# Layer 0's modulation as TensorE sums in 32-column groups, and another order of the steps ahead of the channel mixing

## The chip, the cores and the metric

The kernel runs on one core of a Trainium2 chip. The metric is the device time of one execution in microseconds (us); a kernel's time is the median of several executions. A core has five engines that run side by side, each with its own queue of instructions in program order: TensorE (PE; its weight loads are shown as PEld), VectorE (DVE), ScalarE (ACT), GpSimd (POOL) and SyncE (SP, which here only issues loads and stores). An instruction that waits holds up all that stand behind it on its engine.

## What is computed

A two-layer backbone over 512 latent tokens of 1024 features, with 256 context tokens, in f32. Every layer begins with a modulation: a vector made of the condition `c` (and for the context of `c_ctx`) by a 1024 x 6144 matrix, cut into six chunks of 1024 features: shift, scale and gate of the mixer, then of the MLP.

```python
s_lat = jax.nn.silu(c)
s_ctx = jax.nn.silu(c_ctx)
for i in range(DEPTH):
    mod_l = [m[:, None, :] for m in jnp.split(s_lat @ ada_w[i] + ada_b[i], N_MOD, axis=-1)]
    a_lat = _modulate(_rmsnorm(h_lat, norm1_g[i]), mod_l[0], mod_l[1])      # h * (1 + scale) + shift
    if i % 2 == 0 or ctx_live:
        mod_c = jnp.split(s_ctx @ ada_w[i] + ada_b[i], N_MOD, axis=-1)
        a_ctx = _modulate(_rmsnorm(h_ctx, norm1_g[i]), mod_c[0], mod_c[1])
    ...
    h_lat = h_lat + mod_l[2] * y_lat
    h_lat = h_lat + mod_l[5] * _sq_relu_mlp(
        _modulate(_rmsnorm(h_lat, norm2_g[i]), mod_l[3], mod_l[4]), mlp_w1[i], mlp_w2[i])
return _rmsnorm(h_lat, final_g)
```

`y_lat` is the mixer's output: in layer 0 differential attention beside a Hyena long convolution, in layer 1 a pooling mixer. So layer 0 needs all six chunks for the latent tokens, and chunks 0 and 1 for the context as well.

## The kernel before

Everything is feature-major: tiles of 128 features (partitions) by 512 tokens. Large products are made of f32r parts: each operand is split into a high part (a ScalarE cast) and a low part (a subtraction on VectorE or GpSimd), and three products are summed (`mm3`, `proj_steps`: high x high, high x low, low x high). Products of the modulation are plain f32; TensorE runs each of those as two instructions.

**Stages.** First the start: the Hyena filter's network and spectrum (`fm`, `ft`, `tp`, `fo`, `kp`, `ks`), layer 0's modulation, and the norm and modulation of x (`sq`, `aq`, `xn`, `xm`, then the parts `xh` and `xl`). Then layer 0's mixer: projections (`u`, four products a step, six steps a unit, weights loaded by `x` and split by `w` and `r`), values (`vm`), context keys (`kx`), scores and softmax (`S`, `M`, `E`, `C`), the weighted values (`T`, `H`, `L`, `V`), the transforms of the long convolution (`F`, `I`), and the first output products (`X`). Last the channel mixing: output projection, the MLP of layer 0, the pooling mixer and the MLP of layer 1, one weight tile of 128x1024 after the other.

**What sets the order.** Ahead of the channel mixing the order is written out by hand: the lists START and MIDDLE name one step after another, and `play` emits them; each engine runs its own instructions in that order. A step's name is that of its function, then its number, then sometimes a letter for the engine of an elementwise step (v: VectorE, g: GpSimd). Data dependences and buffers that are still in use become waits.

**Layer 0's modulation.** `sil` holds silu of the condition (columns 0 to 7) and of the context's constant (8 to 15). For the first 512 features of chunks 1 and 0, both streams go over TensorE: `gemv` (`gv`, L594) takes the two columns of one feature tile as stationary operand and 512 weights as moving one, two products a step, eight steps, into two accumulators of two rows; `ga` copies them, `gt` transposes them to columns, `gm` adds bias and gain. All other features go over VectorE: a row step multiplies 128 rows of the transposed weights (`adaT`, 128x1024) by the condition, broadcast over the partitions (`sbc`, made by `sb` and `sc`), and sums along the row (L637: eight `gr` steps in the start; L649: 32 `rw` steps in the mixer, of which eight are the context's). Each is followed by one or two one-column steps for bias and gain (`gf`, `rf`; L250, L255, L660, L665). Chunk 5 of layer 0 and all of layer 1 are such rows in the channel mixing (`grow`, L1472): 8 + 48 of them, one or two after each MLP tile.

The weight tiles and rows come by `lg` and `lr`, half a megabyte each, on SP's queue; the `sraw` ring of four buffers is shared by `lr` rows, raw projection weights (`x`) and later loads. PSUM has two accumulators each of the kinds `mm` and `tr` (512 columns) and two wide ones, `sc` (1024 columns), for filter taps, spectra, scores and the inverse transform.

Of the kernel before, what the change touches and what calls it, by code (L numbers as in the profile page):

```python
# [9 lines left out]
F32 = mybir.dt.float32  # L10
# [8 lines left out]
P = 128  # L19
# [24 lines left out]
MIDDLE = """
ca4g w2 r2 kw3 cs0 j0 sc3 k0 l0 rw0 lr2 nw0 lr3 x3 u12 u13 u14 cr0 rw1 u15 x4 u16 j1 k1 lv0 lr4 w3 rf1 cp0 rf0 rw2
u17 cn0 rw3 r3 ck0 cx2v cx3v cm2 lr5 u18 u19 u20 u21 u22 rf3 cx6v j2 rf2 w4 cx7v rw4 k2 lr6 x5 cx4 rw5 rf5 rf4 r4 l1
l2 cx0 u23 u24 u25 cx5v cm4 cm3 j3 w5 u26 u27 cx1 rw6 u28 k3 rf6 lr8 rw8 rf8 cm0 cm1 x6 lr7 r5v cm6 ch3 rw7 u29 u30
u31 u32 u33 u34 rf7 x7 lr9 ch2 cl2g l3 lb0 ch0 j4 ch6 w6 k4 cl0 x8 rw9 r6 cm7 w7 r7 u35 vm0 vm1 vm2 vm3 lr12 lr10
lr11 j5 k5 ch1 rf9 va0 cl3 vm4 vm5 vm8 cl6 rw10 rf10 vm6 vm7 ch4 w8 cl1 ch7 va1 vh0 cm5 cl4g r8 vm9 rw11 rf11 rw12
rf12 vm10 ch5 cl5 vm12 x9 vm11 cl7g vl0g va2 lr13 w9 vh1 r9 lr14 lr15 x10 w10 vm13 vm14 vm15 vh2 vm16 rw13 lr20 lo0  # L50
rf13 lr18 va3 vm17 vm18 vm19 lr16 vm20 vm21 rw14 rf14 va4 rw15 lr17 lr19 vh3 vm24 vm25 vm26 x11 vm27 lr21 va6 rf15
lr22 x12 vm22 vm23 va5 l4 vl1g vl2g vl3 vm28 vm29 vm30 vh6 vm32 vm31 rw16 vl6 va7 vh7 vm33 vm34 vh4 vm35 va8 r10
rf16 rw17 vl7g vm36 rf17 vm37 vm38 vm39 rw18 rf18 va9 vh5 vm40 rw19 rf19 rw20 rf20 vm41 vh8 vm44 vm45 l5 vl4 vm42
vl5g vm43 vh9 vm46 w11 va10 vm47 u60 u61 vl8g va11 rw21 rf21 rw22 r11 vl9 rf22 vh10 lr24 lr28 lr23 lr25 u62 u63 u64
u65 ka0 lr26 kb0 rw23 km0 rf23 kx0 u66 u67 kx1 u68 u69 u70 u71 w12 ky0 r12 rw24 kd0 rf24 rw25 vl10g kh0 rw26 u72 ka1
kb1 rf25 km1 x13 lr27 x14 x15 lr29 kl0 rw27 rf26 u73 kx2 kx3 u74 u75 u76 kx4 u77 vh11 w13 ky1 r13 kd1 kh1 kl1g rf27
rw28 rf28 kx5 ka2 kb2 ky2 lr30 lr31 rw29 rf29 la0 la1 w14 le0 u78 u79 u80 u81 u82 u83 vl11g km2 r14 rw30 ln0 kd2
rw31 q0 s0 t0 u84 u85 u86 kx6 u87 u88 kh2 w15 kl2 r15 a0 rf30 b0 c0 rf31 b1 c1g u89 kx7 ka3 kb3 km3 S0 M0 x20 x17
u90 u91 S1 M1 u92 S3 kd3 u93 S2 u94 u95 x16 E0 w16 ky3 E1 kh3 r16 kl3g M3 C0 M2 q1 E2 s1 u96 T0 H0 E3 w17 L0 t1 r17
C1 u97 u98 u99 S5 u100 a1 M5 S4 u101 M4 u102 T1 u103 u104 S6 E5 j16 k16 x19 x18 w18 H1 L1 V0 S7 E4 C2 T2 u105 M6 M7  # L60
u106 b2 b3 O0 c2 H2 E7 E6 L2 C3 u107 c3v Q0 r18 u108 S8 f0 f1 T3 u109 M8 j17 H3 L3 w19 E8 S9 u110 u111 M9 k17 E9 Q2
f2 l16 l17 f3 Q3 S10 V1 u112 S11 M10 C4 T4 E10 Q5 r19 O1 M11 E11 H4 w20 S12 M12 u113 q2 u114 u115 Q1 u116 S13 u117
N0 C5 L4 s2 t2v R0 M13 W0 r20 T5 u118 u119 B0 H5 E13 L5 a2 D0 z1 x21 w21 x22 V2 U0 j19 b5 E12 k19 f4 l19 C6 G0 c5 Q4
v0 O2 b4 S14 u120 u121 S15 u122 T6 y0 M14 E14 Q7 c4 H6 K0 f5v p1 r21 M15 E15 L6 u123 u124 u125 S16 C7 S17 M16 M17 T7
q3 s3 x23 u126 u127 u128 U1 E16 H7 L7 V3 E17 w22 v1 C8 O3 t3v Q8 f6 y1 a3 b7 f7v S18 M18 u129 S19 T8 H8 u130 M19 E18
E19 L8 u131 N1 U3 r22 Q6 p0 R1 C9 v3 w23 S20 U2 F2 S21 W1 v2 j21 T9 y3 M20 y2 k21 r23 E20 b6 M21 P2 H9 E21 L9 z0 S23
# [1955 lines left out]
```

## Time and profile before

| | |
|---|---|
| median of the runs shown (3) | 1159.12 us (1159.09 to 1161.04) |
| span of the profiled execution | 1157.6 us |
| TensorE busy | 1098.5 us (95%) |
| VectorE busy | 729.7 us (63%) |
| ScalarE, GpSimd busy | 442.8 us (38%), 455.5 us (39%) |
| loaded and stored | 165.6 MB |

The time outside the span is 1.5 us against the median. Busy shares over the whole span mix stages with different limits: the start and the mixer take the first 352 us, the channel mixing the other 806. So the trace is read by stage, and inside a stage by what ended an engine's idle time. On TensorE a product's listed duration includes the time until its last column is out; products that follow each other overlap in this, so the distance of two starts tells what a product costs in a row of them.

### The profile page before, as it was taken

To read this page: it belongs to the slowest core of one execution; us is meant where nothing else is said; L and a number is where in the kernel's file an instruction comes from. 1 tells how busy PE (TensorE), PEld (TensorE's weight loads), DVE (VectorE), ACT (ScalarE), POOL (GpSimd) and SP (SyncE) were. 2 spreads that over 40 slices of the span, in tenths; PEclk is the share of its full clock that TensorE was granted. 3 is DMA by queue.
4 is the path that set the end of the run, shared out by engine and by line. 5 is a ranking of instruction groups with operands and counts; after the bars stand their busy time and mean duration, and the time that the engine had idled before them with its cause. 6 is when DMAs were issued, how large, how long until landed. Compare 5 with 4: busy or idle time off the path is not lost.

```text
span 1157.6 us, 14600 instructions
## 1 busy us (share of the span) xinstructions
PE 1098.5 (95%) x5624; PEld 917.5 (79%) x5624; DVE 729.7 (63%) x1080; ACT 442.8 (38%) x747; POOL 455.5 (39%) x325
## 2 busy tenths in 40 slices
PE   8788987999999999999999999989999999999996
PEld 2467976787789987888888888989888888888886
DVE  5889887899984768578577666576522332332334
ACT  3555224666535443143133133366422422322331
POOL 5858757655664413113113212356131131231212
PEclk9899998999999899999999999989999999999998
DMA  9577743102625237656646644221231332322302
GB/s 351 206 249 239 246 170 129 55 20 82 186 91 198 74 113 274 232 165 223 242 155 227 224 164 164 73 74 50 97 114 69 110 109 73 109 101 81 105 5 73
DMA packets 49802, 165.55 MB, mean 143 GB/s; under 512 B 5378, under 2 KB 8706, under 8 KB 49604
## 3 DMA queue, kind: packets, MB, share of 16 engines
q1 hardware_dynamic: 47284, 154.13, 38.6%
q0 software_dynamic: 2448, 10.49, 2.7%
q8 instruction: 44, 0.72, 0.3%
q14 instruction: 26, 0.21, 0.1%
HBM read 160.40 MB, written 4.20 MB: 142 GB/s over the span
## 4 chain that ended last, share of the span: by engine, by line
PE 73%; DVE 15%; POOL 4%; ACT 3%; issue 3%; DMA 2%; SPq 0%; POOLq 0%; DVEq 0%; ACTq 0%
PE r L199 11%; PE r L196 10%; PE r L194 10%; PE f L199 9%; PE f L196 9%; PE f L194 9%; PE v L897 2%; DVE mx L1074 1%; DVE g L649 1%; DVE e L1094 1%; DMA g<-in_adaT 1%; PE f L1631 1%; DVE g L637 1%; DVE nl L1530 1%; DVE ks L985 1%
## 5 line engine op out<-in xcount | busy, mean ns | idle before, releaser
L163 POOL TENSOR_TENSOR wlo<-raw,whi 128x1024 fp32r<-128x1024 f32 x77 | 194.7, 2531 | 527.0 <-ACT whi L162 384.8
L196 PE MATMUL r<-gl,whi 128*128 128x512 f32 (+1 forms) x576 | 207.1, 368 | 2.1 <-DVE gl L1622 2.1
L162 ACT CAST whi<-raw 128x1024 fp32r<-128x1024 f32 x135 | 139.7, 1041 | 179.3 <-PE r L196 151.9
L194 PE MATMUL r<-gh,whi 128*128 128x512 f32 (+1 forms) x576 | 207.3, 368 | 0.0
L194 PE MATMUL f<-nh,whi 128*128 128x512 f32 (+1 forms) x512 | 191.4, 379 | 0.0
L196 PE MATMUL f<-nl,whi 128*128 128x512 f32 (+1 forms) x512 | 191.1, 378 | 0.0
L1543 DVE SCALAR_TENSOR_TENSOR h<-r,mods,h 128x512 f32<-128x512 f32 (+1 forms) x81 | 54.4, 671 | 163.8 <-PE r L199 163.6
L1621 DVE TENSOR_TENSOR r<-r 128x512 f32<-128x512 f32 (+1 forms) x72 | 53.8, 748 | 150.4 <-ACT gh L1620 150.3
L199 PE MATMUL r<-gh,wlo 128*128 128x512 f32 (+1 forms) x576 | 130.2, 368 | 0.0
L1619 ACT ACTIVATE r<-f 128x512 f32<-128x512 f32 (+1 forms) x72 | 39.5, 549 | 236.7 <-PE f L199 235.0
L196 PEld LDWEIGHTS r<-gl,whi 128*128 128x128 f32 x576 | 108.4, 188 | 21.5 <-DVE gl L1622 2.5
L194 PEld LDWEIGHTS r<-gh,whi 128*128 128x128 f32 x576 | 108.3, 188 | 19.2
L199 PE MATMUL f<-nh,wlo 128*128 128x512 f32 (+1 forms) x512 | 121.3, 379 | 0.0
L1472 DVE CUSTOM_DVE_ANT_0 g<-g,sbcl 128x1024 f32<-128x1024 f32 x56 | 117.4, 2097 | 1.7 <-DMA g<-in_adaT 1.7
L199 PEld LDWEIGHTS r<-gh,wlo 128*128 128x128 f32 x576 | 100.5, 188 | 18.9
L194 PEld LDWEIGHTS f<-nh,whi 128*128 128x128 f32 x512 | 96.2, 188 | 19.0
L196 PEld LDWEIGHTS f<-nl,whi 128*128 128x128 f32 x512 | 96.3, 188 | 18.8
L199 PEld LDWEIGHTS f<-nh,wlo 128*128 128x128 f32 x512 | 92.3, 188 | 18.9
L163 DVE TENSOR_TENSOR wlo<-raw,whi 128x1024 fp32r<-128x1024 f32 x58 | 75.9, 1308 | 9.5 <-ACT whi L162 9.5
L194 PE MATMUL u<-ah,whi 128*128 128x512 f32 x160 | 67.0, 419 | 9.5 <-ACT whi L735 4.3
L196 PE MATMUL u<-al,whi 128*128 128x512 f32 x160 | 65.4, 409 | 0.3 <-POOL al L719 0.3
L744 POOL TENSOR_TENSOR wlo<-raw,whi 128x1024 fp32r<-128x1024 f32 x19 | 48.4, 2546 | 9.9 <-ACT whi L735 7.0
(372 smaller groups left out, 1948.5 us busy)
## 6 DMA issues: line engine op xcount, KB each, us to landing
raw<-in_w SPq DMA_DIRECT2D x128, 512.0 KB, 4.4
g<-in_adaT SPq DMA_DIRECT2D x96, 512.0 KB, 4.4
raw<-in_w_hy SPq DMA_DIRECT2D x12, 512.0 KB, 3.9
g<-in_adaN SPq DMA_DIRECT2D x8, 512.0 KB, 8.5
raw<-in_w_qk SPq DMA_DIRECT2D x8, 512.0 KB, 3.5
pth<-in_pth POOLq DMA_DIRECT2D x4, 768.0 KB, 7.8
raw<-in_w_out SPq DMA_DIRECT2D x5, 512.0 KB, 3.6
x<-in_xT SPq DMA_DIRECT2D x8, 256.0 KB, 10.8
```

The lines of the kernel that those rows point to most:

```text
L162: act.copy(out=hi, in_=src)
L163: (lo_eng or dve).tensor_tensor(out=lo, in0=src, in1=f32(hi), op=ALU.subtract)
L194: pe.matmul(ps, wh[:, c], ah[i][:, t0 : t0 + n], start=(i == 0), stop=False)
L196: pe.matmul(ps, wh[:, c], al[i][:, t0 : t0 + n], start=False, stop=False)
L199: pe.matmul(ps, wl[:, i * P : (i + 1) * P], ah[i][:, t0 : t0 + n], start=False, stop=(i == k - 1))
L637: dve.tensor_tensor_reduce(out=g, in0=g, in1=sbc[0], scale=1.0, scalar=0.0, op0=ALU.mult, op1=ALU.add, accum_out=mods[:, 0, c, d : d + 1])
L744: ew(pool if k else dve).tensor_tensor(out=wts[k][1], in0=raws[k], in1=f32(wts[k][0]), op=ALU.subtract)
L897: pe.matmul(pp[:, :256], a, b, start=(k == 0 and e == 0), stop=(k == ND - 1 and e == 2))
L1472: dve.tensor_tensor_reduce(out=gin[k], in0=gin[k], in1=sbc[0], scale=1.0, scalar=0.0, op0=ALU.mult, op1=ALU.add, accum_out=mods[:, layer, ...
L1543: dve.scalar_tensor_tensor(out=hs[d][:, seg], in0=pp[:, :n], scalar=gate[:, d : d + 1], in1=hs[d][:, seg], op0=ALU.mult, op1=ALU.add)
L1619: act.activation(out=r, in_=pp[:, :n], func=AF.Relu)
L1621: dve.tensor_tensor(out=r, in0=r, in1=r, op=ALU.mult)
```

## The change

Layer 0's modulation goes over TensorE entirely. The stationary operand is now 32 columns wide (`sil2`, in which the columns of one feature tile's condition and context stand side by side, and whatever follows them fills the other thirty), and a step multiplies one feature tile (128 rows of the weights in their own layout, `adaN`) by 2048 weights: four products of 512 columns, each into another group of 32 partitions of one accumulator (`gemv_tile`). Eight steps `gv` make chunks 1 and 0 of both streams; sixteen steps `rv` in the mixer make chunks 2 and 3 (`rv0` to `rv7`), then 4 and 5 (`rv8` to `rv15`) in the two halves of one wide `sc` accumulator, which they keep until `ra1` and `ra0` have copied it. `gt` and `rt` transpose a copied accumulator by four 128x128 blocks; `gm` and `rm` add bias and gain for eight tiles at a time. The steps `gr`, `gf`, `rw`, `rf` are gone, and so are the context's broadcast condition and the eight rows of chunk 5 in the channel mixing (`gq`). The condition's broadcast is still made, for layer 1's rows.

START has 213 steps in place of 232, MIDDLE 826 in place of 870; nearly all stand in another place, and some 60 elementwise steps are on another engine (eleven weight low parts `r` go from GpSimd to VectorE, three modulations of x, `xm`, from ScalarE to VectorE). In the new lists the first `u` stands behind `xl0`, thirteen `kp` steps and the first two weight splits (`w0`, `w1`); `rv0` to `rv3` stand among the first six units, `rv4` to `rv11` among the values, `rv12` to `rv14` ahead of the first scores, `rv15` behind the second ones. `proj_steps` and `v_unit` look their weights' parts up later, so that a part may be emitted between two of a unit's steps.

```diff
+    sil2 = per.tile([P, 48], F32, name="sil2", tag="sil2")
+    sil = sil2[:, 0:16].rearrange("p (k s) -> p s k", s=2)
+    e16 = sil2[:, 16:32]
+    nhalf, ones = sil2[:, 32:36], sil2[:, 40:41]
+    dve.memset(sil2[:, 32:48], -0.5)
...
-    gtt = [(c, d) for d in range(4, ND) for c in (1, 0)]
...
-        if k < ND:
-            nc.sync.dma_start(out=gts[k], in_=I["adaN"][k])
-        else:
-            c, d = gtt[k - ND]
-            nc.sync.dma_start(out=gts[k], in_=I["adaT"][0, c * D + d * P : c * D + (d + 1) * P, :])
+        nc.sync.dma_start(out=gts[k], in_=I["adaN"][k // 2, :, k % 2, :])
...
-        nc.sync.dma_start(out=rows_in[k], in_=I["adaT"][0, c * D + j * P : c * D + (j + 1) * P, :])
+        nc.sync.dma_start(out=rows_in[k], in_=I["adaN"][k % 16 // 2, :, 2 + 2 * (k // 16) + k % 2, :])
...
+    gav, gas, gat = {}, {}, {}
+    def gemv_tile(dst, k, srcs):
+        for b in range(4):
+            pe.matmul(
+                dst[32 * b : 32 * b + 32, :], sil2[:, 2 * k : 2 * k + 32], srcs[b // 2][:, b % 2 * T : (b % 2 + 1) * T],
+                start=(k == 0), stop=(k == ND - 1),
+            )
+    def gemv_copy(r, src):
+        gas[r] = m3.tile([P, T], F32, name=nm("gas"), tag="P", bufs=4)
+        act.copy(out=gas[r], in_=src)
+    def gemv_columns(r):
+        t = ps_tr("gat")
+        for i in range(4):
+            pe.transpose(t[:, i * P : (i + 1) * P], gas[r][:, i * P : (i + 1) * P], idn)
+        gat[r] = t.rearrange("p (i c h s) -> p s c h i", i=4, c=2, h=2)
+    def by_half(ap):
+        return ap.rearrange("p (h i) -> p h i", h=2)
     @step("gv")
     def gemv(k):
-        for c in range(2):
-            pe.matmul(
-                lazy(gav, c, lambda: ps_tr("gav"))[0:2, :], sil.rearrange("p (s k) -> p k s", s=2)[:, k, :],
-                gts[k][:, c * T : (c + 1) * T], start=(k == 0), stop=(k == ND - 1),
-            )
+        gemv_tile(lazy(gav, 0, lambda: ps_tr("gav")), k, (gts[2 * k], gts[2 * k + 1]))
     @step("ga")
-    def gemv_out(c):
-        gas[c] = m3.tile([2, T], F32, name=nm("gas"), tag="P", bufs=4)
-        act.copy(out=gas[c], in_=gav[c][0:2, :])
+    def gemv_out(_):
+        gemv_copy(0, gav[0])
     @step("gt")
     def gemv_t(_):
-        gat.append(ps_mm("gat"))
-        for i in range(8):
-            pe.transpose(gat[0][:, 2 * i : 2 * i + 2], gas[i // 4][:, i % 4 * P : (i % 4 + 1) * P], idn[0:2, 0:2])
+        gemv_columns(0)
     csm = per.tile([P, ND], F32, name="csm", tag="csm")
     @step("gm")
     def first_mods(k):
-        gr = gat[0][:, 0:16].rearrange("p (c d s) -> p c s d", c=2, s=2)
-        dst_s, dst_m = ((smul[:, 0, 0:4], mods[:, 0, 0, 0:4]), (csm[:, 0:4], cmods[:, 0, 0:4]))[k]
-        dve.tensor_tensor(out=dst_s, in0=gr[:, 0, k, :], in1=gpre[:, 0, 0:4], op=ALU.add)
-        dve.tensor_tensor(out=dst_s, in0=dst_s, in1=pr("n1g", 0, 4), op=ALU.mult)
-        dve.tensor_tensor(out=dst_m, in0=gr[:, 1, k, :], in1=pr("ada_b", 0, 4), op=ALU.add)
+        gr = gat[0][:, k]
+        dst_s, dst_m = ((smul[:, 0, :], mods[:, 0, 0, :]), (csm, cmods[:, 0, :]))[k]
+        dve.tensor_tensor(out=by_half(dst_s), in0=gr[:, 0], in1=by_half(gpre[:, 0, :]), op=ALU.add)
+        dve.tensor_tensor(out=dst_s, in0=dst_s, in1=pr("n1g", 0, ND), op=ALU.mult)
+        dve.tensor_tensor(out=by_half(dst_m), in0=gr[:, 1], in1=by_half(pr("ada_b", 0, ND)), op=ALU.add)
+    rav = {}
+    @step("rv")
+    def row(n):
+        r, k = n // ND, n % ND
+        acc_ = lazy(rav, 0, lambda: ps_sc("rav"))[:, r * T : (r + 1) * T]
+        gemv_tile(acc_, k, (rows_in[2 * n], rows_in[2 * n + 1]))
+    @step("ra")
+    def row_out(r):
+        gemv_copy(1 + r, rav[0][:, r * T : (r + 1) * T])
+    @step("rt")
+    def row_t(r):
+        gemv_columns(1 + r)
+    @step("rm")
+    def row_mods(r):
+        gr = gat[1 + r][:, 0]
+        o = (2 + 2 * r) * ND
+        if r == 0:
+            pairs = ((mods[:, 0, 2, :], 0), (mods[:, 0, 3, :], 1))
+        else:
+            pairs = ((mods[:, 0, 5, :], 1),)
+            dst = smul[:, 1, :]
+            dve.tensor_tensor(out=by_half(dst), in0=gr[:, 0], in1=by_half(gpre[:, 1, :]), op=ALU.add)
+            dve.tensor_tensor(out=dst, in0=dst, in1=pr("n2g", 0, ND), op=ALU.mult)
+        for dst, c in pairs:
+            dve.tensor_tensor(
+                out=by_half(dst), in0=gr[:, c], in1=by_half(pr("ada_b", o + c * ND, o + (c + 1) * ND)), op=ALU.add
+            )
...
-        sbps[n] = bcast(ps, "mm" if n < 2 else "tr", sil[:, n * 4 : n * 4 + 4], 4, "sb")
+        sbps[n] = bcast(ps, "tr", sil[:, 0, n * 4 : n * 4 + 4], 4, "sb")
...
-        act.copy(out=(sbc[0] if n < 2 else sbc_c)[:, n % 2 * T : (n % 2 + 1) * T], in_=sbps[n])
-    @step("gr")
-    def row0(k):
-        c, d = gtt[k]
-        g = gts[ND + k]
-        dve.tensor_tensor_reduce(
-            out=g, in0=g, in1=sbc[0], scale=1.0, scalar=0.0, op0=ALU.mult, op1=ALU.add, accum_out=mods[:, 0, c, d : d + 1]
-        )
-    @step("gf")
-    def row0_fin(k):
-        ada_fin(0, *gtt[k])
-    @step("rw")
-    def row(k):
-        kind, c, j = rows_q[k]
-        g = rows_in[k]
-        dve.tensor_tensor_reduce(
-            out=g, in0=g, in1=sbc_c if kind == "c" else sbc[0], scale=1.0, scalar=0.0,
-            op0=ALU.mult, op1=ALU.add, accum_out=cmods[:, c, j : j + 1] if kind == "c" else mods[:, 0, c, j : j + 1],
-        )
-    @step("rf")
-    def row_fin(k):
-        kind, c, j = rows_q[k]
-        if kind == "s":
-            ada_fin(0, c, j)
-        elif c == 1:
-            dve.scalar_tensor_tensor(
-                out=csm[:, j : j + 1], in0=cmods[:, 1, j : j + 1], scalar=gpre[:, 0, j : j + 1], in1=pr("n1g", j),
-                op0=ALU.add, op1=ALU.mult,
-            )
-        else:
-            dve.tensor_tensor(out=cmods[:, c, j : j + 1], in0=cmods[:, c, j : j + 1], in1=ada_b(0, 0, j), op=ALU.add)
...
-        act.activation(out=xs[d], in_=xs[d], func=AF.Identity, scale=smul[:, 0, d : d + 1], bias=mods[:, 0, 0, d : d + 1])
+        s_, b_ = smul[:, 0, d : d + 1], mods[:, 0, 0, d : d + 1]
+        if other[0] is dve:
+            dve.tensor_scalar(out=xs[d], in0=xs[d], scalar1=s_, scalar2=b_, op0=ALU.mult, op1=ALU.add)
+        else:
+            act.activation(out=xs[d], in_=xs[d], func=AF.Identity, scale=s_, bias=b_)
...
-    gq = [(0, 5, j) for j in range(ND)] + [(1, c, j) for c in range(6) for j in range(ND)]
+    gq = [(1, c, j) for c in range(6) for j in range(ND)]
```

## Rows read from the trace of the kernel before

**Rows 1.** The page's first line: the profiled execution.
```profile
span 1157.6 us, 14600 instructions
```
**Rows 2.** Busy time by stage; times in us, (x) counts of instructions.
```profile
core 0: us, PE busy (x) PEld busy (x) DVE busy (x) ACT busy (x) POOL busy (x), PEclk, DMA share, GB/s
...
34.40:78.25 43.85, 34.05 (x129) 24.06 (x128) 38.81 (x54) 23.37 (x35) 31.41 (x19) 0.88 0.57 195
78.25:195.54 117.29, 101.15 (x607) 89.31 (x605) 100.64 (x162) 42.57 (x85) 81.20 (x62) 0.97 0.63 212
195.54:352.00 156.46, 147.40 (x837) 126.34 (x838) 137.12 (x225) 88.33 (x191) 97.99 (x94) 0.97 0.29 93
352.00:1157.60 805.60, 788.01 (x3989) 669.90 (x3987) 432.31 (x614) 272.96 (x411) 223.97 (x117) 0.99 0.38 131
```
**Rows 3.** TensorE's waits from 78 to 196 us: total, times, longest.
```profile
PE s L1068 <- ACT qh L1018: 5.4, 1, 5.4
```
**Rows 4.** Groups of VectorE, 34.4 to 195.54 us: count, busy us, mean ns, idle before.
```profile
L649 DVE CUSTOM_DVE_ANT_0 g<-g,sbcl 128x1024 f32<-128x1024 f32 x24 | 32.3, 1346 | 5.6 <-DMA g<-in_adaT 5.6
L637 DVE CUSTOM_DVE_ANT_0 g<-g,sbcl 128x1024 f32<-128x1024 f32 x8 | 13.9, 1760 | 0.0
L649 DVE CUSTOM_DVE_ANT_0 g<-g,sbcc 128x1024 f32<-128x1024 f32 x8 | 12.0, 1513 | 0.1
L255 DVE TENSOR_TENSOR mods<-mods,prm 128x1 f32<-128x1 f32 x20 | 9.6, 479 | 0.4
...
L250 DVE SCALAR_TENSOR_TENSOR smul<-mods,gpre,prm 128x1 f32<-128x1 f32 x11 | 6.7, 610 | 0.1
```
**Rows 5.** TensorE in order of time, start: start us, us, count.
```profile
20.29 3.60 PE L594 MATMUL gav<-g,sil 128*2 128x512 f32 x8
23.82 0.50 PE L494 MATMUL fp<-w3h,hds 128*128 128x512 f32 x1
24.24 0.49 PE L495 MATMUL fp<-w3l,hds 64*128 64x512 f32 x1
```
**Rows 6.** The same view, later in the start.
```profile
45.15 0.40 PE L185 MATMUL kp<-pmh,cs 128*128 128x512 f32 x1
45.38 0.40 PE L186 MATMUL kp<-pml,cs 128*128 128x512 f32 x1
...
45.85 0.60 PE L219 MATMUL sb<-idn,sil 128*128 128x128 f32 x4
...
64.67 0.50 PE L194 MATMUL u<-ah,whi 128*128 128x512 f32 x1 [4.25 <-ACT whi L735]
```
**Rows 7.** Busy time by stretch of 10 us around the end of the first loads.
```profile
30.00:40.00 10.00, 5.57 (x22) 2.52 (x21) 9.49 (x10) 4.98 (x10) 7.62 (x5) 0.89 0.98 391
40.00:50.00 10.00, 9.36 (x38) 7.08 (x39) 7.56 (x10) 3.65 (x5) 8.39 (x6) 0.77 0.19 57
```
**Rows 8.** Groups of VectorE, ScalarE and GpSimd, 0 to 352 us.
```profile
L744 DVE TENSOR_TENSOR wlo<-raw,whi 128x1024 fp32r<-128x1024 f32 x3 | 4.7, 1580 | 0.0
...
L735 ACT CAST whi<-raw 128x1024 fp32r<-128x1024 f32 x22 | 23.2, 1054 | 20.9 <-DMA raw<-in_w_qk 7.0 <-DMA raw<-in_w_hy 5.3 <-PE kc L196 4.9
...
L711 ACT ACTIVATE x<-x,mods,smul 128x512 f32<-128x512 f32 x8 | 6.4, 811 | 8.0 <-DVE mods L255 4.3 <-POOL x L707 3.0 <-DVE x L707 0.8
...
L715 ACT CAST ah<-x 128x512 fp32r<-128x512 f32 x8 | 4.7, 609 | 0.0
...
L558 ACT ACTIVATE sp<-kp 128x1024 f32<-128x1024 f32 x4 | 4.1, 1016 | 0.5 <-DMA spec<-sp 0.5
...
L744 POOL TENSOR_TENSOR wlo<-raw,whi 128x1024 fp32r<-128x1024 f32 x19 | 48.4, 2546 | 9.9 <-ACT whi L735 7.0 <-DMA raw<-in_w_hy 2.8
...
L719 POOL TENSOR_TENSOR al<-x,ah 128x512 fp32r<-128x512 f32 x3 | 6.8, 2290 | 6.5 <-ACT ah L715 6.5
```
**Rows 9.** The largest group of VectorE in the channel mixing.
```profile
L1472 DVE CUSTOM_DVE_ANT_0 g<-g,sbcl 128x1024 f32<-128x1024 f32 x56 | 117.4, 2097 | 1.7 <-DMA g<-in_adaT 1.7
```

More of the change, by code (lines that the diff above doesn't have):

```diff
@@ L48 @@
[L48 to L52, printed above, removed]
@@ L127, in body @@
     make_identity(nc, idn)
-    nhalf = per.tile([P, 4], F32, name="nhalf", tag="nhalf")
-    dve.memset(nhalf, -0.5)
-    ones = per.tile([P, 1], F32, name="ones", tag="ones")
+    sil2 = per.tile([P, 48], F32, name="sil2", tag="sil2")
[3 more added lines that the diff above has]
+    dve.memset(sil2[:, 32:48], -0.5)
     dve.memset(ones, 1.0)
@@ L226, in norm_bcast @@
         return bcast(ps_pool, tag, r, n, "nb")
-    def ada_tile(sbc, layer, chunk, j, dst):
-        g = st.tile([P, D], F32, name=nm("g"), tag="sraw", bufs=4)
-        dma = nc.sync.dma_start(out=g, in_=I["adaT"][layer, chunk * D + j * P : chunk * D + (j + 1) * P, :])
-        red = dve.tensor_tensor_reduce(
-            out=g, in0=g, in1=sbc, scale=1.0, scalar=0.0, op0=ALU.mult, op1=ALU.add, accum_out=dst
-        )
-        if layer:
-            tc.keep_in_program_order(dma)
-            tc.keep_in_program_order(red)
     def ada_b(layer, chunk, j=None):
@@ L268, in ps_sc @@
         return ps.tile([P, 1024], F32, name=nm(name), tag="sc", bufs=2)
-    def sil_bcast(k, name, sb=None):
-        if sb is None:
-            sb = gm.tile([P, D], F32, name=nm(name), tag="sbc", bufs=1)
-        for h in range(2):
-            bp = bcast(ps, "tr", sil[:, k * 8 + h * 4 : k * 8 + h * 4 + 4], 4, "sb")
-            act.copy(out=sb[:, h * T : (h + 1) * T], in_=bp)
-        return sb
     hx = ExitStack()
@@ L380, in w_load @@
         raws[k] = wfetch(mix_w[k])
-    rows_q = [("c", c, d) for d in range(4, ND) for c in (1, 0)]
-    rows_q += [("s", c, j) for c in (2, 3, 4) for j in range(ND)]
     @step("lr")
     def row_load(k):
-        kind, c, j = rows_q[k]
         rows_in[k] = st.tile([P, D], F32, name=nm("g"), tag="sraw", bufs=4)
-        nc.sync.dma_start(out=rows_in[k], in_=I["adaT"][0, c * D + j * P : c * D + (j + 1) * P, :])
+        nc.sync.dma_start(out=rows_in[k], in_=I["adaN"][k % 16 // 2, :, 2 + 2 * (k // 16) + k % 2, :])
     ftr = per.tile([P, 2], F32, name="ftr", tag="ftr")
     dve.tensor_scalar(out=ftr, in0=pr("f1", 0, 2), scalar1=1.0 / (2 * math.pi), scalar2=None, op0=ALU.mult)
-    e16 = per.tile([P, 16], F32, name="e16", tag="e16")
     act.activation(out=e16, in_=prm[:, 0:16], func=AF.Exp, scale=-1.0)
@@ L891, in v_unit @@
         pp = lazy(vps, n, lambda: ps_mm("v"))
[L892 removed]
+        ws = [w if isinstance(w, list) else w_halves(w) for w in wts[6 + 2 * pn + g // 2]]
         for k in range(2 * g, 2 * g + 2):
[L894 removed]
+            wh, wl = (x[k % 4 // 2][:, k % 2 * 256 : (k % 2 + 1) * 256] for x in ws)
             mm3_ = ((lh[k], wh), (ll[k], wh), (lh[k], wl))
```

94 lines of the change are left out of this document (45 added, 49 removed).

## The prediction

> **What bounds the kernel now.** The profiled execution spans 1157.6 us [rows 1]; the median of the three runs shown is 1159.1, 1.5 us more, so 1.5 us is added to every sum on the span. I read the busy time by stage first, with cuts at 34.4 us (the transposed first sums), 78.25 (end of the second projection unit), 195.54 (first scores) and 352 (channel mixing) [rows 2]. The channel mixing takes 805.6 us with TensorE busy 788.0 of them: nothing that the change does on another engine shortens it. Ahead of it the picture is another one. From 34.4 to 195.54 VectorE is busy 139.5 of 161.1 us, more than TensorE with 135.2; from 195.54 to 352 TensorE has 147.4 of 156.5 and VectorE 137.1.
>
> Then the waits of TensorE, to see what its idle time hangs on: from 78.25 to 195.54 it idles 16.1 us, and the longest wait, 5.4 us, is for a ScalarE cast that stood behind VectorE work [rows 3]. Last the groups of VectorE in the stretch where it leads [rows 4]: the largest are the modulation rows, 32.3, 13.9 and 12.0 us, and the one-column steps behind them, 9.6 and 6.7 us. These 74.5 us are what the change takes away, over half of VectorE's 139.5 us there.
>
> **What the change adds on TensorE.** Layer 0's sums become 24 tile steps (8 `gv` ahead of the projections, 16 `rv` among them), each of four products of 128x32 by 512 columns, plain f32, one per group of 32 columns. The trace of before has 16 products of this kind with two columns (`gav`); each shows as two instructions on TensorE, and eight of them take 3.60 us, 0.43 us apart [rows 5]. All of these go to the same column group, so they can't show whether different groups run side by side. That is the unknown price, and I bound it from both sides by these rows:
> - One after the other: 8 x 0.43 = 3.4 us a step.
> - All four groups at once: 2 x 0.43 = 0.86 us a step.
> - Side by side, but started in program order: a product's second instruction needs the columns that its first still streams through, and the next group's first instruction stands behind that second one. So the second of one group runs beside the first of the next, and a step takes 5 x 0.43 = 2.14 us.
>
> To each a change of form is added. In [rows 5] products of 128 and of 64 rows alternate and start 0.42 us apart, though products of the same columns in one form start 0.23 apart [rows 6]: 0.2 us at each change, 0.4 in and out of a lone step. A step then costs 3.8, 2.5 or 1.25 us. A gain by this alone is excluded, since no row shows a product taking less than its columns.
>
> The Trainium skill, page "TensorEngine Tiling (Array Packing)", section "Key Properties", says that changing the tiling mode drains TensorE; the trace agrees, with the 0.2 us just named. Its page "TensorE: Matmul & The Clock Gate", Part 3, has column tiles running concurrently, three of them 2.38 times as fast as in turn, and matmuls beginning and ending strictly in order; by its factor alone a step would be some 1.5 us (an estimate from that page), and no run here shows it yet.
>
> I take 2.5 us: the emission order of the two instructions is in the code, and [rows 5] show that two instructions on the same columns never overlap. I keep 1.25 and 3.8 for the range.
>
> **Up to 78.25 us (start): -9 us.** The bytes loaded ahead of the sums are the same: 16 half-megabyte weight tiles in place of eight and eight rows. The loads run at 391 GB/s until 40 us, and then fall to 57 [rows 7], so the last weight tile lands at about 40 us in either kernel. The eight new tiles of `gv` are 8 x 2.5 = 20 us on TensorE, against 13.7 (32 instructions of 0.43) now; they begin when the second tile has landed, at about 20 us, and the last waits for the last load. With its 2.1 us, a copy and four transposes (0.6 us, [rows 6]), the modulation of all eight feature tiles is known at 43.5 us. Before, four of them hung on eight VectorE rows of 1.76 us [rows 4]. What is late next is ScalarE's queue, in the new order: two weight splits (1.05), three modulations (0.81), three high parts (0.61) and two spectrum copies (1.02) and one of half that width before the last of the first unit's high parts, some 9 us [rows 8], then a low part on GpSimd (2.29). First projection at 55 us, against 64.7 [rows 6]. Twelve projection steps of four products (12 x 4 x 0.23 = 11.0) and three spectrum steps that are queued among them (3 x 0.7) bring the second unit's end to 69 us, against 78.25: -9. The conditions' broadcast (`sb`, `sc`), halved, no longer stands ahead of the sums.
>
> **78.25 to 352 us (mixer): +21 us.** Sixteen `rv` steps at 2.5 us add 40.0 us, and eight transposes (two of 0.6 us for four, [rows 6]) 1.2. They stand on an engine that is busy 248.6 of these 273.8 us, and so mostly on the path. Against that stands what TensorE can win back: its idle time, 16.1 + 9.1 us, and some 4 us in which it runs at the lower clock level (granted 0.97 over both stages). VectorE loses the 32 rows (44.3 us) and their one-column steps; the new order fills part of the room with eleven weight splits from GpSimd (1.58 instead of 2.55 us each, [rows 8]), which also frees the raw buffers earlier. After the change VectorE has some 65 of 135 us of work ahead of the first scores, so there its waits vanish, all but 6 us of the casts' chains; behind the first scores the softmax and transform work is the same, and VectorE stays near nine tenths busy. I give back 14 + 6 = 20 us. Sum: 40.0 + 1.2 - 20 = +21.
>
> The moved loads: 32 half-megabyte tiles are loaded for `rv`, as 32 rows were before, by the same queue and into the same ring of four buffers. Each `rv` waits for two of them, and behind it on TensorE wait projections that don't need them; where the queue is late by one load, an `rv` costs some 2 to 4 us more. One load a step is no more than before, so I put this at nothing, covered by the 6 us left above. The sums of `rv` also keep one of the two wide accumulators until the second scores; the order puts four to six projection steps between the first two scores, which covers a maximum and an exponential.
>
> **Channel mixing: 0.** Eight rows fewer (2.1 us each, [rows 9]) and 4 MB less to load, beside a TensorE that is busy 98% there. The rows that are left start at the same place and end eight places earlier.
>
> Sum: -9 + 21 = +12 on 1157.6, and 1.5: **1171 us**.
>
> **The rivals.** First, **the groups run all at once** (1.25 us a step). TensorE then gains 20 us in the mixer against my sum, and 1.5 us in the start: 1149 us, faster than before. For it: four outputs on separate partitions, separate weights. Against: two instructions of one product share their columns. It decides below some 1.75 us a step, where 16 x 0.75 eats the 12 us.
> Second, **the groups don't run side by side** (3.8 us): 16 x 1.3 = 21 us more in the mixer, and the eight `gv` (30 us from the first pair's landing) pass the loads and put the modulation at 54 us, 11 us more: 1204 us. For it: no product of before overlaps another.
> Third, **waits of the new order**: a price as in my forecast, but row loads that come late for five or more of the sixteen `rv`, 3 us each, 15 us: 1186 us. For it: each step wants two loads out of a ring of four, shared with the projections' weights. Against: the loads fill only 212 GB/s of that stage [rows 2].
> That nothing of this matters (VectorE was never the limit, and the price is hidden) would leave 1159; TensorE's 90% share of the mixer speaks against a hidden price.
>
> **How the numbers follow.** My forecast 0.45, all at once 0.27, in turn 0.18, late loads 0.10. Around each I allow some 7 us for what the order wins or loses. The range is 1145 to 1203: it takes in most of the first two rivals and leaves out their far halves. The measurement tells 0.2% (2.3 us) from no change. Faster: nine tenths of the first rival and a tenth of my forecast, 0.30. Within 0.2%: 0.07. Slower: 0.63, whose own range is 1162 to 1203.
>
> **What would show it.** The price: in the new sums' rows on TensorE, starts of neighbouring groups a few ns apart or 0.43 us apart, and 0.86, 2.1 or 3.4 us for the eight instructions of a step. The start: a first projection at 55 us. The room: TensorE's idle time from the first projections to the first scores at 6 us, and VectorE some 65 us busy there. I am wrong if the step's price is below 1.75 us, or if TensorE's idle time stays as it was with VectorE half empty: then other chains than VectorE's held it.

## The result and the profile after

The changed kernel takes 1139.4 us (median of four runs, 1138.9 to 1141.4) against 1159.9 on the same chip: 0.9826 of it, 95% interval 0.9807 to 0.9845. The forecast was 1171, slower. The profiled execution after has a span 19.6 us shorter than that of [rows 1]:

```profile
span 1138.0 us, 14758 instructions
```

To see where the 19.6 us went, both traces are cut at the same events: the first projection product, the first score, the first product of the channel mixing's own projection, and one 37 to 39 us behind that. First the kernel before (64.67 us is the time in [rows 6]), then the one after; columns as in [rows 2], the mean granted clock is the third number from the end.

```profile
64.67:195.54 130.87, 114.28 (x654) 99.09 (x654) 112.06 (x181) 52.60 (x100) 91.16 (x68) 0.96 0.66 223
195.54:358.31 162.77, 153.71 (x864) 131.57 (x865) 139.74 (x229) 93.50 (x199) 100.19 (x95) 0.97 0.30 98
358.31:397.71 39.40, 37.18 (x270) 35.77 (x268) 22.07 (x39) 17.50 (x31) 19.30 (x11) 0.94 0.25 94
397.71:1157.60 759.89, 744.52 (x3693) 628.90 (x3692) 407.63 (x571) 250.30 (x374) 202.47 (x107) 0.99 0.38 132
```

```profile
62.23:186.72 124.49, 123.82 (x753) 95.33 (x751) 60.70 (x95) 50.30 (x95) 48.57 (x55) 1.00 0.60 208
186.72:342.29 155.57, 153.50 (x916) 133.51 (x913) 124.23 (x222) 96.11 (x203) 103.76 (x109) 1.00 0.36 118
342.29:379.42 37.13, 34.91 (x270) 33.50 (x268) 21.95 (x38) 18.23 (x32) 18.32 (x10) 1.00 0.30 100
379.42:1138.00 758.58, 742.92 (x3694) 626.21 (x3692) 389.43 (x548) 250.59 (x374) 204.63 (x108) 0.99 0.38 127
```

The start gives 2.4 us (64.67 to 62.23), the two mixer stages 6.4 and 7.2, the first stage of the channel mixing 2.3, the rest 1.3. In the mixer TensorE's idle time falls from 25.6 us (16.6 + 9.1) to 2.7 (0.7 + 2.1), and its clock from 0.96 and 0.97 to 1.00, worth some 10 us (0.04 x 130.87 + 0.03 x 162.77), if TensorE had work throughout the slow stretches. Against these 33 us stand sixteen `rv` steps, 16 us, their transposes, 1.2, and nine spectrum products (2.1) that now follow the first projection: 33 - 19.3 = 13.7, measured 13.6. VectorE does 60.7 us of work ahead of the first scores where it did 112. TensorE's waits of over 0.1 us, from the transposes of the first sums (48.6 us) to the channel mixing, are all in these four rows (the answer to [rows 3]):

```profile
PE gat L576 <- ACT gas L570: 2.9, 1, 2.9
PE rav L563 <- DMA g<-in_adaN: 1.7, 1, 1.7
PE u L196 <- DVE al L704: 0.5, 1, 0.5
PE wt L1098 <- DVE rs L1146: 0.3, 1, 0.3
```

The new step itself, one `rv` between a projection step and column sums (TensorE in order of time; start us, us):

```profile
74.69 1.52 PE L200 MATMUL u<-ah,wlo 128*128 128x512 f32 x6
76.14 1.06 PE L563 MATMUL rav<-g,sil 128*32 128x512 f32 x8
77.14 0.61 PE L214 MATMUL nt<-sil,cssq 128*128 128x1 f32 x4
```

Its eight instructions hold the engine for 1.0 us (76.14 to 77.14); the forecast had 2.5.

### The profile page after: what moved, and what is told of

Read it like the earlier page. It is cut to its first block, busy times and chain, and to the rows that moved or that the text cites. A ratio compares the mean times of both kernels' runs of the same rounds, so it can differ in the third digit from the quotient of the medians.

```text
span 1138.0 us, 14758 instructions
## 1 busy us (share of the span) xinstructions
PE 1100.1 (97%) x5780; PEld 908.6 (80%) x5780; DVE 634.7 (56%) x952; ACT 441.4 (39%) x743; POOL 404.3 (36%) x317
## 4 chain that ended last, share of the span: by engine, by line
PE 84%; DVE 4%; ACT 1%; POOL 1%; DMA 1%; issue 1%; POOLq 0%; SPq 0%; ACTq 0%; DVEq 0%
PE r L200 11%; PE r L196 11%; PE r L194 11%; PE f L200 9%; PE f L196 9%; PE f L194 9%; PE v L882 3%; PE u L200 3%; PE u L194 2%; PE u L196 2%; PE rav L563 1%; DVE nl L1515 1%; PE wt L1098 1%; PE s L1053 1%; PE s L1054 1%; PE f L1616 1%
## 5 line engine op out<-in xcount | busy, mean ns | idle before, releaser
L163 POOL TENSOR_TENSOR wlo<-raw,whi 128x1024 fp32r<-128x1024 f32 x77 | 195.0, 2536 | 521.3 <-ACT whi L162 377.5
L1457 DVE CUSTOM_DVE_ANT_0 g<-g,sbcl 128x1024 f32<-128x1024 f32 x48 | 98.5, 2053 | 1.6 <-DMA g<-in_adaT 1.6
L194 PE MATMUL u<-ah,whi 128*128 128x512 f32 x160 | 64.0, 400 | 0.0
L196 PE MATMUL u<-al,whi 128*128 128x512 f32 x160 | 62.8, 393 | 0.5 <-DVE al L704 0.5
L1477 ACT ACTIVATE sq<-h 128x256 f32<-128x256 f32 (+1 forms) x47 | 21.3, 459 | 79.0 <-DVE h L1528 78.8
```

The source lines that it names most:

```text
L163: (lo_eng or dve).tensor_tensor(out=lo, in0=src, in1=f32(hi), op=ALU.subtract)
L194: pe.matmul(ps, wh[:, c], ah[i][:, t0 : t0 + n], start=(i == 0), stop=False)
L196: pe.matmul(ps, wh[:, c], al[i][:, t0 : t0 + n], start=False, stop=False)
L1457: dve.tensor_tensor_reduce(out=gin[k], in0=gin[k], in1=sbc[0], scale=1.0, scalar=0.0, op0=ALU.mult, op1=ALU.add, accum_out=mods[:, layer, ...
L1477: act.activation(out=sq, in_=hs[d][:, seg], func=AF.Square)
```

## The experiments

Times are medians of all runs. "Mixer" is the length from the first projection product to the first product of the channel mixing's projection in the profiled execution, "idle" TensorE's idle time in it. The kernels ran on several chips; the kernel before took 1159.9 to 1161.4 us beside them, so differences of under 2 us between two rows say nothing.

| kernel | us | mixer | idle |
|---|---|---|---|
| before | 1159.9 | 293.6 | 25.6 |
| after | 1139.4 | 280.1 | 2.7 |
| one_group | 1176.1 | 316.2 | 1.1 |
| pairs | 1153.1 | 291.1 | 1.9 |
| alternate | 1148.4 | 290.2 | 2.5 |
| no_products | 1130.0 | 269.7 | 6.8 |
| before_short_rows | 1146.2 | 277.6 | 15.1 |
| rows_new_order | 1162.0 | 303.9 | 35.1 |
| rows_order_own | 1162.4 | 300.8 | 32.9 |
| sums_old_order | 1180.2 | 318.6 | 25.2 |
| old_order_dve_splits | 1184.8 | 326.8 | 30.3 |
| old_order_late_sums | 1176.8 | 319.3 | 25.2 |
| new_then_old | 1160.1 | 298.5 | 15.9 |
| old_then_new | 1173.1 | 312.6 | 22.8 |
| splits_gpsimd | 1146.4 | 285.9 | 5.6 |
| spectrum_first | 1139.2 | 279.5 | 2.5 |

### The price of a step

In all three kernels the products of an `rv` step get other groups of columns; `start` and `stop` follow the group's first and last product.

```diff
-        gemv_tile(acc_, k, (rows_in[2 * n], rows_in[2 * n + 1]))
+        for b in range(4):
+            a = 32 * (k % 4)                     # one_group
+            a = 32 * ((2 * k + b // 2) % 4)      # pairs
+            a = 32 * ((2 * k + b % 2) % 4)       # alternate
+            pe.matmul(acc_[a : a + 32, :], sil2[:, 2 * k : 2 * k + 32], ...
```

> The changed kernel, but each `rv` step's four products go to one group of 32 columns (another one at each step) instead of one product to each group; so the sums behind layer 0's gates and second norm come out mixed. Eight instructions of 0.43 us can then not run side by side: 3.4 us and 0.14 around them, 3.58 a step, against 1.0 in the changed kernel. Theory A (TensorE has no idle time left in the mixer, so every step's price counts in full): 16 x 2.58 = 41 us more than the changed kernel, 1181 us. Rival B (other chains are close behind and TensorE still has room): the longer steps are partly hidden, under 25 us more, below 1165.

> The changed kernel, but of a `rv` step's four products the first two go to one group of columns and the last two to another (groups change from step to step; sums mixed as in one_group). It asks in which order the two instructions of each product run. If each column group takes its products one after the other and a second instruction holds up nothing in another group, a third product still stands behind the second in the queue: starts at 0, 0.43, 0.86 (second product, and with it the third), 1.29, 1.72, 2.15: 2.58 + 0.14 = 2.72 us a step, 16 x 1.72 = 27 us more than the changed kernel, 1167. If all first instructions of a step are taken before all second ones: 2.15 + 0.14 = 2.29 a step, 21 us more, 1160. If the instructions run strictly in the order of the products, as the prediction had it: 3.0 + 0.14 a step, 34 us more, 1174. This step price is near the 2.5 us of the prediction, so the run also shows what the rest of its sum was worth.

> As pairs, but the four products alternate between the two column groups. Two side by side, twice: 1.72 + 0.14 = 1.86 us a step, 16 x 0.86 = 14 us more than the changed kernel, 1153, whether each group has its own queue or all first instructions come first. Strictly in the order of the products: 2.15 + 0.14 = 2.29 a step, 21 us more, 1160.

Measured: 1176.1, 1153.1 and 1148.4 us. One step of one_group in order of time:

```profile
74.61 3.62 PE L612 MATMUL rav<-g,sil 128*32 128x512 f32 x8
78.16 0.60 PE L214 MATMUL nt<-sil,cssq 128*128 128x1 f32 x4
```

These are the starts of the eight instructions of one step in the records of the four traces, in us from the first one, and the start of what follows:

```
after      0.000 0.007 0.013 0.020 0.453 0.460 0.467 0.473   next 0.996
alternate  0.000 0.006 0.453 0.460 0.882 0.889 1.311 1.318   next 1.841
pairs      0.000 0.013 0.453 0.466 0.882 0.895 1.311 1.325   next 1.847
one_group  0.000 0.453 0.882 1.311 1.741 2.170 2.599 3.028   next 3.551
```

In one group the eight follow each other 0.43 us apart, as in [rows 5]; with four groups four start within 20 ns, and their second instructions 0.45 us later. `pairs` settles in which order: its program gives products 1 and 2 to one group and then 3 and 4 to another, and yet an instruction of the second group starts 13 ns after the first. So product 3 did not stand behind product 2, which had to wait for its group; none of the three orders that were written down for `pairs` (2.29, 2.72 and 3.1 us a step) held, all were too long. In these traces the groups behave as separate queues. The Trainium skill, page "TensorE: Matmul & The Clock Gate", Part 3, has matmuls start and end strictly in program order; `pairs` shows a start out of it. For the time: 2.55 us more a step (one_group) made the kernel 36.7 us longer where 41 were expected, 0.85 us more made it 13.7 and 9.0 longer where 13.6 is 16 steps' worth. Rival B of one_group (under 25 us more) falls. Theory A, that the price counts in full, holds to between three quarters and nine tenths: the mixer alone is 36.1 us longer where 40.9 are 16 steps' worth (one_group), and 11.0 and 10.1 where 13.6 are (`pairs`, `alternate`).

### Without the products

The products of the steps with `k` over 0 are left out:

```diff
-        gemv_tile(acc_, k, (rows_in[2 * n], rows_in[2 * n + 1]))
+        if k == 0:
+            gemv_tile(acc_, 0, (rows_in[2 * n], rows_in[2 * n + 1]), 1)
```

> The changed kernel without the products of 14 of the 16 `rv` steps (those of the first tile of each half stay; the rows are still loaded, and the gates and second norm come out wrong). Theory A (TensorE is the only limit from the first projections on): 14 x 1.0 = 14 us less than the changed kernel, 1125. Rival B (VectorE, casts or loads stand close behind): less than 6 us is won, 1133 to 1139, and TensorE shows new waits in the mixer.

1130.0 us, 9.4 less than the changed kernel: between the two. The mixer is 10.4 us shorter. TensorE's longest waits there, new against the kernel after:

```profile
PE v L883 <- DVE v L889: 2.9, 2, 2.5
PE us L185 <- DMA b<-in_dfw: 1.6, 1, 1.6
PE s L1055 <- POOL ql L1014: 0.7, 1, 0.7
```

So about 10 of the 14 us taken away were on the path, and some 4 turn into waits for VectorE, a transform's load and GpSimd: the next limit is not far behind.

### VectorE's relief, the order, and both

The change does two things at once, and each can be had without the other. `before_short_rows` is the kernel before with its 32 rows cut to 8 columns: relief with no price and no new order.

```diff
-            out=g, in0=g, in1=sbc_c if kind == "c" else sbc[0], scale=1.0, scalar=0.0,
+            out=g[:, 0:8], in0=g[:, 0:8], in1=(sbc_c if kind == "c" else sbc[0])[:, 0:8], scale=1.0, scalar=0.0,
```

> The kernel before, with the 32 VectorE rows that stand among the projections cut to their first 8 columns (so part of the context's modulation, the gates and the second norm come out wrong); loads, one-column steps and the order stay. It takes some 40 us of VectorE work away and puts nothing on TensorE. Theory A (the rows made TensorE wait, and its sparse stretches cost it the clock): the idle 25 us and most of the 10 us of slow clock between the first projections and the channel mixing come back, 1160 - 30 = 1130 us. Rival B (other chains of the old order held TensorE just as much, and the new order won the time): 1150 or above.

1146.2 us: it wins 14, neither 30 nor nothing. All of it lies ahead of the first scores; behind them the stage takes 162.2 us as in the kernel before. The edit frees more than VectorE: GpSimd's same 68 instructions ahead of the first scores take 72.0 us instead of 91.2, the low parts of the values 0.48 us each instead of 0.82 (`vl`), those of their weights 1.33 instead of 1.84 (`wv`). So part of what the rows cost may have come by way of GpSimd, which no run separates. The stages ahead of and behind the first scores:

```profile
66.42:181.80 115.38, 110.26 (x654) 97.38 (x655) 78.73 (x181) 52.51 (x100) 71.99 (x68) 0.97 0.72 253
181.80:344.04 162.24, 152.31 (x864) 129.76 (x865) 141.00 (x229) 93.44 (x199) 100.97 (x95) 0.98 0.29 98
```

The new order with the rows on VectorE, in the place of each `rv`:

```diff
-        gemv_tile(acc_, k, (rows_in[2 * n], rows_in[2 * n + 1]))
+        for k in (2 * n, 2 * n + 1):
+            g, c, j = rows_in[k], 2 + k // ND, k % ND
+            dve.tensor_tensor_reduce(out=g, in0=g, in1=sbc[0], ..., accum_out=mods[:, 0, c, j : j + 1])
+            ada_fin(0, c, j)
```

> The changed kernel and its order, but the rows of chunks 2 to 5 summed on VectorE again: at the place of each `rv` step two rows and their one-column steps (three places are a few steps later or earlier, so that no queue locks), no copies and transposes for them. The whole computation is kept. VectorE gets some 32 x 1.4 + 32 x 0.45 = 59 us more, TensorE some 17 us less than in the changed kernel. Theory A (VectorE's relief is the gain): TensorE idles some 20 us and loses clock again, 1150 to 1160 us. Rival B (the new order is the gain and would carry the rows too): 1125 to 1135, better than both kernels.

It loaded another layer's rows; with layer 0's own:

> rows_new_order, now with layer 0's own weights as rows (rows_new_order loaded the same bytes of another layer's, so its values differed). The same order and work on each engine, so the same time is expected by every theory, 1157 to 1165 us; TensorE idle some 35 us between the first projections and the channel mixing.

1162.0 and 1162.4 us, as slow as before (1.0014 of it, 1.0001 to 1.0027), with more idle time on TensorE than before:

```profile
PE v L897 <- DVE v L903: 15.2, 4, 7.3
PE s L1069 <- DVE ql L1028: 4.7, 1, 4.7
PE v L897 <- DVE u L851: 3.0, 1, 3.0
PE u L204 <- DVE x L851: 2.3, 1, 2.3
```

Every one of these waits is for VectorE: the new order by itself is worth nothing, rival B falls; theory A's 1150 to 1160 us was 2 us short. One reservation: the new order as it stands has eleven low parts and three modulations of x on VectorE, beside the rows here; the new order with the rows and with those steps off VectorE was not run. Last the sums on TensorE in the old order. The second list of steps is that of before, with `rv n` where `rw 2n` or `rw 2n+1` came last, and `ra`, `rt`, `rm` behind the eighth of each half:

```diff
-... cr0 rw1 u15 x4 u16 j1 k1 lv0 lr4 w3 rf1 cp0 rf0 rw2 u17 cn0 rw3 r3 ...
+... cr0 rv0 u15 x4 u16 j1 k1 lv0 lr4 w3 cp0 u17 cn0 rv1 r3 ...
```

> The changed kernel with the order of before from the second projection stage to the end of the mixer: each `rv` step stands where the second of its two rows stood, the copies, transposes and column steps a few steps behind the last of them; splits that stood on GpSimd stand there again. The whole computation is kept. Theory A (taking the rows off VectorE is enough): TensorE is as free of idle time as in the changed kernel, 1139 to 1144 us. Rival B (the new order was needed for half of the gain or more): 1150 or above.

1180.2 us, 20 slower than before: theory A is 36 us too low, and rival B's 1150 or above holds, though it did not speak of a loss. TensorE idles as much as in the kernel before, 25.2 us, only on other things (first the stage ahead of the first scores, then TensorE's waits, then two of SP's queue):

```profile
62.57:218.22 155.65, 139.09 (x800) 104.48 (x798) 58.14 (x85) 51.16 (x100) 71.18 (x71) 0.94 0.55 183
...
PE rav L573 <- DMA g<-in_adaN: 13.3, 4, 5.2
PE s L1063 <- ACT qh L1013: 2.3, 1, 2.3
PE av L195 <- DVE wt L1124: 2.1, 1, 2.1
PE wt L1108 <- DVE e L1089: 2.0, 5, 0.6
...
SPq L182 <- POOL wlo L739: 34.1, 7, 6.1
SPq L369 <- PE rav L573: 33.0, 10, 5.2
```

The sums wait for loads, and the loads, on SP's queue, for buffers that GpSimd's low parts and the sums themselves hold. VectorE is no longer the reason: ahead of the first scores it is busy 58.1 of 155.7 us. So the mixer is 25 us longer by the 19.3 us of added TensorE work and some 4 us more of lower clock, and nothing is won back. SP's waits alone don't tell this: in the changed kernel the same two are not much shorter, and TensorE waits 1.7 us for its sums:

```profile
SPq L172 <- POOL wlo L729: 26.4, 5, 6.5
SPq L359 <- PE rav L563: 23.1, 9, 4.7
```

### What the old order lacks

Two single changes to `sums_old_order`: eleven splits from GpSimd to VectorE as in the new order (`r2` to `r2v` and so on), or nine sums (not eight, as the expectation has it) moved back by 3 to 24 steps of the list.

> sums_old_order, with eleven weight low parts moved from GpSimd to VectorE as in the new order, and nothing else. In sums_old_order four `rv` steps waited 13.3 us for their loads, and the loads stood on SP's queue behind weight loads that waited for buffers which GpSimd's low parts still held (34 us and 20 us of such waits). Theory L (the loads were late because GpSimd held the buffers): the four waits shrink to under 4 us together, and with the clock 1160 to 1167 us. Rival O (the places of the loads and sums in the old order make them late): the waits stay and the time is 1174 to 1181.

> sums_old_order with eight of the sixteen `rv` steps moved back, so that at least 6 us of other TensorE work stands between the later of a step's two loads and the step (before the move four had 0 to 4 us there; the loads take 4.1 us to land). Nothing is left out. Theory L (in the old order TensorE meets the sums before their loads have landed, and that is the cost of the old order ahead of the first scores): the 13.3 us of waits shrink to under 4 and the clock comes back, 1160 to 1168 us. Rival R (the ring of four buffers is the limit: a later sum frees its two buffers later and the next loads start later): the waits move to other steps, 1174 or above.

1184.8 and 1176.8 us. The splits' engine was not it: five sums wait 16.3 us, theory L falls, and the time lies above rival O's 1181 as well. Moving the sums back halves their waits, but others come up, and rival R, not L, gives the time:

```profile
PE rav L573 <- DMA g<-in_adaN: 6.6, 2, 3.9
PE wt L1108 <- DVE e L1089: 4.6, 5, 2.4
PE v L892 <- ACT wv L727: 2.5, 1, 2.5
PE gat L586 <- ACT gas L580: 2.0, 1, 2.0
...
SPq L182 <- PE rav L573: 24.1, 6, 8.7
```

That `SPq L182`, a weight load, waits 24.1 us for `rav` where it waited 11.7 in sums_old_order fits rival R: a later sum frees its two buffers later, and the weights of the next projections queue behind. A larger ring was not tried. Then each half of the order alone, exchanged at the first score step `S0`:

> The changed kernel, with the new order up to the first scores and from there on the steps that are left in the order of before (as in sums_old_order). Nothing is left out. Theory F (nearly all that the new order is worth lies ahead of the first scores): 1139 to 1143 us. Rival G (the two halves count each for itself; behind the first scores the old order took 162.2 to 163.0 us in three kernels with rows or sums, the new one 155.6): some 7 us more than the changed kernel, 1145 to 1149, with the old waits of TensorE for softmax and transform steps back.

> The opposite of new_then_old: the old order with the sums on TensorE up to the first scores, the new order behind. Theory F: as sums_old_order, 1178 to 1182 us. Rival G: some 7 us less than sums_old_order, 1171 to 1175, and from the first scores on TensorE idles under 4 us.

1160.1 and 1173.1 us. Behind an old half the new order of the second half is worth 7 us (1180.2 to 1173.1; the stage takes 155.4 us), as rival G said (TensorE idles 4.4 us there, not under 4), behind a new one 21 (1160.1 to 1139.4). The new first half is worth 20 with the old half behind it and 34 with the new one. So new_then_old came out 11 us above the upper end of rival G, and theory F fell by more: the gain lies in both halves, and some 14 us of it only in the two together. The old half wants 25 more steps done by the first scores, among them the last sum, both sets of transposes and two projection steps (in new_then_old TensorE has run 800 instructions by then, against 753 after). In this version they stand in a block ahead of `S0`, and behind it TensorE idles 11.0 us, in the changed kernel 2.1; that too little is left to put beside the softmax is read from the order, not tested:

```profile
60.85:199.14 138.29, 133.36 (x800) 102.34 (x799) 68.56 (x107) 54.42 (x104) 54.53 (x59) 0.98 0.60 210
199.14:359.38 160.24, 149.25 (x867) 127.95 (x865) 139.80 (x224) 91.54 (x196) 96.46 (x91) 1.00 0.29 98
```

Which of the steps that moved ahead of the scores win the 20 us was not separated further.

### Two details of the new order

Splits on GpSimd again (`r2v` to `r2` and so on, twelve steps of the second list); and `kp2 kp3 ny0` ahead of `gt0` in the first list.

> The changed kernel, with its twelve weight low parts (`r` with a v, in the second list) back on GpSimd, at the same places of the order: 12 x 1.3 us off VectorE, 12 x 2.5 us on GpSimd. Theory A (what VectorE's room is used for counts: the low parts come late from GpSimd): TensorE waits again for weights, 3 to 8 us more than the changed kernel, 1142 to 1147. Rival B (GpSimd had the time): 1139, no change.

> The changed kernel with three spectrum steps (kp2, kp3 and ny0) on TensorE's queue ahead of the transposes of the first sums (gt0) instead of behind them. TensorE idled 2.9 us there, waiting for ScalarE's copy. Theory A (from the transposes on TensorE is the only limit): the idle time is filled and 2 to 2.9 us are won, 1136.5 to 1137.5. Rival B (the modulation behind the transposes is the limit): it comes as much later as the steps outlast the wait, and nothing is won, 1139 to 1141.

With the splits back on GpSimd 1146.4 us: 7 more, theory A, 5.6 of them behind the first scores (161.2 us). The room on VectorE is used. spectrum_first takes 1139.2 us (1137.4 to 1140.8), not to be told from the changed kernel. In its trace the wait of 2.9 us is filled and the channel mixing starts 1.7 us earlier (340.61 against 342.29), but the next 38.3 us, 37.1 after, run at a clock of 0.96, which takes 1.2 of it back. No version with the whole computation beats the changed kernel by more than runs differ.

## Why the prediction was wrong

**The price, 24 of the 32 us.** The term that failed is the 2.5 us a step (five times 0.43, and 0.4): a second instruction was held to stand in front of the next group's first. A step takes 1.0 us. The two outer cases were right in kind and a little high (1.25 and 3.8; measured 1.0 and 3.55). The point from which it decides, 1.75, was too low: `pairs` and `alternate` at 1.85 us a step are still 0.7 and 1.0% faster than before. The first rival, all at once, is what happened, though its 1149 us is 10 too high, since it kept the 20 us of the next paragraph; of [rows 5], all in one group, nothing could be read on it, and the choice between the bounds rested on an argument from program order, which `pairs` contradicts. What a step takes beyond 2 x 0.43, the change of form, is 0.14 us, not 0.4.

**What TensorE wins back, 13 us.** Forecast 20, measured 33 (22.9 idle, some 10 clock): idle time ahead of the first scores 0.7 us where 6 was said. VectorE's 60.7 us of work there had been put at 65. The "some 4 us" of lower clock was misread: a clock of 0.97 over 273.8 us costs 8 (0.03 x 273.8). But the reason given, that its room ends the waits, is half of it: relief alone won 14 us (before_short_rows), the order alone nothing (rows_order_own), sums in the old order lost 20, and only both together 20 the other way. Behind the first scores VectorE was said to stay near nine tenths busy; it is busy 124.2 of 155.6 us, and with the sums on TensorE the new order makes this stage 7 us shorter (old_then_new).

**The late loads.** The third rival was put at 1186 us with a chance of 0.10. In the new order its mechanism costs 1.7 us; in the old one it is real, 13.3 us, and that kernel takes 1180.

**The start, some 7 us in the other direction.** Forecast -9 at the end of the second unit, measured -2.1 (78.25 to 76.14). The modulation came at 50.2 us, not 43.5, and the first projection at 62.23, not 55:

```profile
SPq L321 <- PE gav L563: 12.7, 4, 6.4
...
42.34 3.36 PE L563 MATMUL gav<-g,sil 128*32 128x512 f32 x24
44.65 0.14 PEld L563 LDWEIGHTS gav<-g,sil 128*32 128x32 f32 x4 [0.29 <-DMA g<-in_adaN]
48.60 1.11 PE L576 MATMUL gat<-idn,gas 128*128 128x128 f32 x4 [2.90 <-ACT gas L570]
...
62.23 0.39 PE L194 MATMUL u<-ah,whi 128*128 128x512 f32 x1
...
47.45 0.62 ACT L503 CAST pmh<-pv 128x512 fp32r<-128x512 f32 x1 [5.77 <-DVE pv L498]
47.97 0.58 ACT L570 COPY gas<-gav 128x512 f32<-128x512 f32 x1
...
58.74 1.02 ACT L529 ACTIVATE sp<-kp 128x1024 f32<-128x1024 f32 x1 [1.42 <-PE kp L523]
59.66 1.65 ACT L700 CAST ah<-x 128x512 fp32r<-128x512 f32 x3
...
60.35 2.55 POOL L704 TENSOR_TENSOR al<-x,ah 128x512 fp32r<-128x512 f32 x2 [3.18 <-ACT ah L700]
```

The step that failed is when the modulation is known. The last weight tile was put at about 40 us; the sums' last four instructions wait for it until 44.65. SP's queue, which issues these loads, waits 12.7 us in the start for buffers that earlier sums still hold. The last sum ends at 45.7, and its copy stands on ScalarE behind a cast that waits for VectorE until 47.45. From there on the length was right, 11.5 us in the forecast and 11.4 from 50.2 to 61.65, when GpSimd has the low part that the first step's second product needs, but in part by luck: the two weight splits (2.0 us) ran before the modulation, and 3.2 us of ScalarE's waits for spectrum products came in their place. TensorE's own queue, which was not followed, holds eleven spectrum steps and the highest frequency's product behind the transposes and is busy with them until 62.23, so the two limits end 0.6 us apart.

**Channel mixing.** Forecast 0, measured -3.6 us. 2.3 us of it lie in its first 37 us, where the clock shows 1.00 instead of 0.94. It does not follow the change: kernels with the new order show there 0.94 (pairs), 0.96 (alternate, splits_gpsimd, spectrum_first) and 1.00 (after, one_group, no_products), with 39.3 to 37.1 us. What decides it stays open. (The four figures of these paragraphs run between slightly different events and sum to 34 us, not 32.)

## What to carry to other kernels

Four f32 products of 128x32 by 512 columns in four 32-column groups can be priced at little more than one product's time (1.0 us here, against 3.55 in one group), not at a chain of their instructions; a price that decides a forecast and that no row shows deserves the wider bound, not an argument. Taking work off a busy engine and reordering the rest are not two gains to be added: here the sums alone lost 20 us, the order alone won nothing, and both together won 20. When a step is moved on to the engine that sets the time, look at the loads that it waits for: on VectorE the rows waited 5.6 us for theirs [rows 4], on TensorE in the old order the sums wait 13.3 us, and in the new one 1.7. Which places in the order make the difference was not found; moving the sums alone did not do it.

## What the runs showed of the hardware

Column groups don't wait for each other: a product whose group is busy doesn't hold up one for a free group behind it (13 ns, `pairs`; shown for two and four groups of 32 columns). When the load of a step's second half comes late, its first half runs before: one step ahead of the projections shows four instructions at 37.51 us and four at 39.34.

In the first 34 us of the changed kernel products run at about half speed: this pair starts 0.72 us apart, that of [rows 5] 0.42, and eight sum instructions hold 1.93 us against 1.06 later. The rows of both kernels print a granted clock of 1.00 there, but that is no measurement: the changed kernel's trace has its first clock record at 34.9 us, that of before at 10.5, and a stretch without a record is printed as 1.00. By the durations it is the lower level, 1.2 GHz. TensorE had been busy 6.8 of the first 20 us, before the change 14.7. The slower filter taps stand ahead of the first sums, which start at 25.8 us where the forecast had 20; how much of the late loads in the start comes from this was not tested.

```profile
20.00 0.79 PE L465 MATMUL fp<-w3h,hds 128*128 128x512 f32 x1
20.73 0.79 PE L466 MATMUL fp<-w3l,hds 64*128 64x512 f32 x1
...
25.79 1.93 PE L563 MATMUL gav<-g,sil 128*32 128x512 f32 x8
```
